# Channel-first partition order for the packed tap operand of a Conformer convolution (32 instead of 4 as the outermost dimension of its reads)

## The chip, the cores and the metric

The kernel runs on one core of a Trainium2 chip. The metric is the device time of one execution in microseconds (us), the median of several runs; lower is better. A second number, the span, is what the hardware profiler covers of one execution from its first to its last instruction.

## What is computed

A small diffusion backbone with two layers, one sequence of 1024 latent tokens and 256 context tokens, model width 1024, all in float32. Layer 0 mixes tokens with a Conformer convolution, layer 1 with windowed attention; each layer ends in a gated convolutional feed-forward part. Every sub-layer is preceded by an RMS norm and by shift, scale and gate values (the modulation, "ada" in the kernel), which are matrix products of the condition vectors. The change lies in the Conformer part:

```python
def conformer_conv(h, w_pw1, b_pw1, w_dw, b_dw, ln_g, ln_b, w_pw2, b_pw2):
    u = h @ w_pw1 + b_pw1
    a, g = jnp.split(u, 2, axis=-1)
    v = a * jax.nn.sigmoid(g)
    v = dwconv(v, w_dw, b_dw)              # per channel, 31 taps along the tokens
    v = jax.nn.silu(layernorm(v, ln_g, ln_b))
    return v @ w_pw2 + b_pw2
```

## The kernel before, in words

Channels lie on the 128 partitions, so the width of 1024 is 8 blocks of 128 ("channel" below means such a block, `c` from 0 to 7), and tokens lie along the free dimension: two tiles of 512 latent tokens (t = 0 and 1) and one of 256 context tokens (t = 2). Float32 products are made of three matmuls of a high and a low part (`mm3`, line 193); weights arrive in a tile `raw`, are split by ScalarE into `wh` (line 914) and by VectorE into `wl` (line 919).

The convolution stage is one loop over the channels (lines 988 to 1061), written out by hand: in `tc.manual_schedule` the order of the code is the order on TensorE, VectorE, ScalarE and GpSimd. The transfers, all issued by SyncE (SP), are ordered by a scheduler instead, and SP works its list strictly in order. A turn of the loop for channel `c` does this:

- It computes GLU of the next channel, `c + 1`, for the three token tiles: `glu_mm` on TensorE for the gate and the value half, `glu_gate` on ScalarE, `glu_mul` on VectorE, which writes the padded row `v`.
- The 31 taps of channel `c` are shared out. `NPE` of them (8 for channels 0 to 5, then 16 and 28) go to TensorE (`pe_taps`, matmuls at line 822), `NDV` (13, 13, 13, 13, 13, 13, 8, 0) to VectorE (`dve`, line 843), and the rest are products on ScalarE (line 848) added by GpSimd (line 849). VectorE adds onto what TensorE left in the accumulator `cacc`; `last` (line 853) adds the GpSimd part and frees `cacc`, of which there is one, for the next channel.
- For TensorE a matmul contracts over 128 partitions: 32 channels times 4 shifts of the token row. So that four shifted copies of a row stand on different partitions, `Shifted.load` (lines 795 to 805) stores `v` to a DRAM tile `v_dram` (line 799) and reads it back with four copies (line 792), one for each group of 32 channels, each with 4 shifts. The tile `vp` takes the front of the rows, `vpb` their end. The store of t = 0 is followed by reads into `vp`, that of t = 1 by more of `vp`, that of t = 2 by the reads into `vpb`. Each read waits on SP for its store to have landed.
- A modulation block of the layer is computed beside it (`ada_steps`): four pairs of matmuls (line 211), each with a 512 KB load of its own (`ld_ada`, line 109, into one of two `raw` buffers that the weight loads `w_load` use too), then a copy, transposes (line 223, the step `fin`) and a reduction on VectorE (line 226).

The source pattern of the reads is built here, with the shift outside and the channel inside:

```python
def rows_of(t, pitch, first, shift, n):
    return bass.AP(t.tensor, t.offset + first, [[shift, 4], [pitch, 32], [1, n]])
```

Partition 32 r + m therefore holds shift r of channel m. The tap weights must stand in the same order: `load_taps` (line 629) reads them with the same helper and a shift of 0, and `pack_taps` (line 638) picks with 12 ScalarE copies of 32 partitions each (line 647) the taps of each shift into `wpk`. Before the first channel's GLU, the prologue (lines 922 to 986) runs norm and modulation and packs the taps. The loaded tap tile has the buffer (`tag="vp"`) that the first reads into `vp` then take.

Of the kernel before, what the change touches and what calls it, by code (L numbers as in the profile page):

```python
# [8 lines left out]
F32 = mybir.dt.float32  # L9
# [9 lines left out]
P = 128  # L19
D = 1024  # L20
KC = D // P
# [8 lines left out]
TAPS = 31  # L30
# [5 lines left out]
NPE = (8, 8, 8, 8, 8, 8, 16, 28)  # L36
# [7 lines left out]
SEG = {}  # L44
# [4 lines left out]
NPAR = _o  # L49
# [3 lines left out]
def hybrid_dit_kernel(  # L53
# [4 lines left out]
    nc = tc.nc  # L58
# [31 lines left out]
    ident = const.tile([P, P], F32, name="ident")  # L90
# [291 lines left out]
    x = [None] * 3  # L382
# [208 lines left out]
    shift = pool(xst1, "shift", side="right")  # L591
# [17 lines left out]
    with ExitStack() as cs:  # L609
# [4 lines left out]
        cv = pool(cvs, "cv", 2)  # L614
# [3 lines left out]
        OOF = (0, 512, SEQ + PADW)  # L618
        rbt = pc.tile([P, 1536], F32, tag="cv", name="rbt")
        id4 = cv.tile([P, 32], F32, name="id4", bufs=1)  # L620
        nc.vector.tensor_reduce(out=id4, in_=ident.rearrange("p (r m) -> p m r", m=32),
                                axis=AX.X, op=ALU.add)
        wpk = cv.tile([P, SUM_M, 4], F32, name="wpk", bufs=1)

        def rows_of(t, pitch, first, shift, n):

            return bass.AP(t.tensor, t.offset + first, [[shift, 4], [pitch, 32], [1, n]])

        def load_taps():

            o, n = SEG["wdw"]
            w = cv.tile([P, 4, n], F32, tag="vp", name="wdw4", bufs=1)
            for g in range(4):
                nc.sync.dma_start(out=w[:, g],
                                  in_=rows_of(par, NPAR, 32 * g * NPAR + o, 0, n))
            return w

        def pack_taps(w):
            c0 = 0
            while c0 < KC:  # L640
                m = NPE[c0] // 4
                n = sum(x == NPE[c0] for x in NPE[c0:])
                o = sum(NPE[:c0]) // 4
                for r in range(4):
                    rows = slice(32 * r, 32 * r + 32)
                    src = w[rows].rearrange("p g (c t) -> p c t g", t=TAPS)
                    nc.scalar.copy(
                        out=wpk[rows, o:o + n * m, :].rearrange("p (c s) g -> p c s g", s=m),
                        in_=src[:, c0:c0 + n, m * r:m * r + m, :])
                c0 += n  # L650

        def ada_src(b, ks):
            return adaw[0, b, :, ks, :]
# [79 lines left out]
        def glu_mm(q, t, half, part=None):  # L733
            n = TOK[t][1]
            if part in (None, 0):
                q.ps[half] = pc.tile([P, 512], F32, tag="s", name="glu_ps", bufs=2)
            ops = unit_ops((q.wg, q.wa)[half], *x[t])
            if part is not None:
                ops = ops[4 * part:4 * part + 4]
            mm3(q.ps[half][:, :n], ops, part is not None, part in (None, 0), part in (None, 1),  # L740
                t == 2)
# [7 lines left out]
        def glu_mul(q, t):  # L749
            n = TOK[t][1]  # L750
            nc.vector.scalar_tensor_tensor(out=q.v[:, VOF[t]:VOF[t] + n], in0=q.ps[1][:, :n],
                                           scalar=seg("bpw1", q.c, 1), in1=q.sg[:, :n],
                                           op0=ALU.add, op1=ALU.mult)
# [111 lines left out]
        def run(steps, n):  # L865
            for _ in range(min(n, len(steps))):
                steps.pop(0)()
# [54 lines left out]
        with tc.manual_schedule(engines=CONV_ENGINES):  # L922
            load_next(True)
            stats(0)
            ada0(2)
            bcast_a(0)
            bcast_b(0)
            normalize_h(0)
            ada0(0)
            load_next(True)  # L930
            load_block(1)
            load_h(2, nc.sync)
            w4 = load_taps()
            apply(0, 0, 2)
            stats(1, nc.vector, 0, 4)
            apply(0, 2, 4)
            split_pending()
            split_pending()
            q = glu_begin(0)
            ada0(3)  # L940
            stats(1, nc.vector, 4, 8)
            glu_mm(q, 0, 0, 0)
            stats(2, nc.vector, 0, 4)
            stats(2, nc.vector, 4, 8)
            bcast_a(1)
            ada0(1)
            bcast_a(2)
            bcast_b(1)
            apply(0, 4, 6)
            apply(0, 6, 8)  # L950
            glu_mm(q, 0, 1, 0)
            glu_mm(q, 0, 0, 1)
            normalize_h(1)
            glu_mm(q, 0, 1, 1)
            apply(1, 0, 2)
            glu_out(q, 0)
            apply(1, 2, 4)
            bcast_b(2)
            glu_mm(q, 1, 0, 0)
            normalize_h(2)  # L960
            apply(1, 4, 6)
            apply(1, 6, 8)
            apply(2, 0, 4)
            apply(2, 4, 8)
            pack_taps(w4)
            dgs = tap_weights(0)
            glu_mm(q, 1, 1, 0)
            glu_mm(q, 1, 0, 1)
            glu_mm(q, 1, 1, 1)
            w_load()  # L970
            w_load()
            vp = Shifted(0, q.v)
            vp.load(0)
            glu_out(q, 1)
            vp.load(1)
            wh = w_hi()
            glu_mm(q, 2, 0)
            w_lo(wh)
            glu_mm(q, 2, 1)
            glu_out(q, 2)  # L980
            vp.load(2)
            w_lo(w_hi())
            ys = [make_h(t, "y") for t in range(3)]

            ld_ada(0, 0)
            ld_ada(0, 1)
            fin = None
            for c in range(KC):
                wide_taps = M[c] * P > 256
                if wide_taps:  # L990
                    dgs = tap_weights(c)
                r, taps = pe_taps(c, vp, dgs)
                first, pq, dq, last = conv_steps(c, q.v, r, NPE[c], NDV[c])
                ada_ps = pc.tile([P, 512], F32, tag="s", name="ada_ps", bufs=2) if c == KC - 1 else None
                ada = ada_steps(0, 4 + c, lambda u, c=c: araw[c, u], ada_ps)
                if c + 1 < KC:
                    q = glu_begin(c + 1)
                    glu_mm(q, 0, 0)
                    glu_gate(q, 0)
                    glu_mm(q, 0, 1)  # L1000
                    run(ada, 2)
                    ld_ada(c, 2)
                    ld_ada(c, 3)
                    run(taps, 4)
                    glu_mul(q, 0)
                    if fin:
                        fin()
                    first()
                    run(pq, 2)
                    vp = Shifted(c + 1, q.v)  # L1010
                    vp.load(0)
                    if c > 0:
                        ymean(c - 1)
                    glu_mm(q, 1, 0)
                    run(pq, 1)
                    glu_gate(q, 1)
                    run(ada, 2)
                    w_load()
                    w_load()
                    run(dq, 3)  # L1020
                    run(pq, 1)
                    glu_mm(q, 1, 1)
                    run(ada, 1)
                    run(dq, 3)
                    glu_mul(q, 1)
                    vp.load(1)
                    run(pq, 1)
                    if M[c + 1] * P <= 256:
                        dgs = tap_weights(c + 1)
                    wh = w_hi()  # L1030
                    glu_mm(q, 2, 0)
                    run(dq, 1)
                    w_lo(wh)
                    ld_ada(c + 1, 0)
                    run(pq, 1)
                    glu_gate(q, 2)
                    wh = w_hi()
                    glu_mm(q, 2, 1)
                    run(dq, 1)
                    glu_mul(q, 2)  # L1040
                    vp.load(2)
                    w_lo(wh)
                    ld_ada(c + 1, 1)
                    run(pq, 99)
                    run(dq, 99)
                    fin = ada.pop()
                else:
                    run(ada, 2)
                    ld_ada(c, 2)
                    ld_ada(c, 3)  # L1050
                    fin()
                    first()
                    run(pq, 99)
                    ymean(c - 1)
                    run(taps, 2)
                    run(ada, 3)
                    for i in range(4):
                        load_ada(i)
                    run(taps, 2)
                    run(dq, 99)  # L1060
                last()
# [3 lines left out]
        with tc.manual_schedule(engines=CONV_ENGINES):  # L1065
# [159 lines left out]
            for t in range(3):  # L1225
                n = TOK[t][1]
# [69 lines left out]
            for u in range(2, 2 * KC):  # L1296
                g, dc = divmod(u, KC)
                tiles = tiles_of(u)
                w = unit(("pw2", g, dc), 0)
# [534 lines left out]
```

## Time and profile before

| | before |
|---|---|
| device time, median of 3 runs | 2856.61 us (2853.77 to 2858.43) |
| the profiled execution, device time | 2854.5 us |
| its span | 2852.7 us |
| TensorE matmuls busy in the span | 2669.1 us, 94% |
| VectorE, ScalarE, GpSimd busy | 56%, 34%, 19% |
| chain that ended last: TensorE | 75% |
| chain that ended last: DMA | 9% (`vpb<-v_dram` 3%, `v_dram<-v` 3%) |

The page's chain is followed back from the last instruction: each piece is the work, or the wait, that released the next. TensorE carries three quarters of it, mostly in the two feed-forward parts. [...] The DMA share is the mean busy share of the core's 16 DMA engines. In a row of the timeline the bracket gives the idle time of that engine before the instruction and what ended it.

### The profile page before, as it was taken

What the parts mean: (1) busy time and instruction counts of PE and PEld (TensorE: products, weight loads), DVE (VectorE), ACT (ScalarE), POOL (GpSimd) and SP (SyncE); (2) the same over time, 40 slices, a digit from 0 to 9 for tenths busy, and PEclk for the clock granted to TensorE, in tenths of its full rate; (3) what the DMA queues carried; (4) which work ended last, traced back from release to release, by engine and by line L of the source; (5) the groups of instructions that cost most, each with busy time, mean ns of one, the idle gap of its engine ahead of it and who ended that gap; (6) DMA issues with size and microseconds to landing.
All of it is one profiled execution on the core that took longest, in us unless ns stands there. A gap on an engine that the chain in (4) does not pass through costs nothing.

```text
span 2852.7 us, 34110 instructions
## 1 busy us (share of the span) xinstructions
PE 2669.1 (94%) x13860; PEld 2155.7 (76%) x13860; DVE 1609.8 (56%) x2273; ACT 984.0 (34%) x1405; POOL 549.7 (19%) x384
## 2 busy tenths in 40 slices
PE   5888784999999999999999999899999999999997
PEld 3556561577888888888888788788878888888886
DVE  6346452545445445544544866998975455545546
ACT  6333321555221111222112524777752222222223
POOL 1365641332000000000000402556630000000003
PEclk8899997999999999999999999999999999999998
DMA  6444464532111111111111163233011111111111
GB/s 238 122 138 136 138 193 149 192 109 83 59 45 37 37 38 37 38 38 45 37 37 38 49 210 111 55 85 78 22 54 59 45 52 45 52 45 52 45 52 67
DMA packets 79421, 225.53 MB, mean 79 GB/s; under 512 B 8480, under 2 KB 20384, under 8 KB 76960
## 3 DMA queue, kind: packets, MB, share of 16 engines
q1 hardware_dynamic: 79264, 223.36, 24.4%
q8 instruction: 109, 1.79, 0.3%
q14 instruction: 48, 0.39, 0.0%
HBM read 202.17 MB, written 21.16 MB: 78 GB/s over the span
## 4 chain that ended last, share of the span: by engine, by line
PE 75%; DMA 9%; DVE 8%; ACT 5%; issue 2%; SPq 1%; POOL 1%; DVEq 0%; ACTq 0%; POOLq 0%
PE up_ps L193 37%; PE dn_ps L193 17%; DMA vpb<-v_dram 3%; DMA v_dram<-v 3%; PE glu_ps L193 3%; PE wo_ps L193 2%; PE pw_ps L193 2%; PE pB L193 2%; PE pA L193 2%; PE cacc L822 2%; PE tp L1545 1%; DVE tl L178 1%; PE v_ps L193 1%; SPq L792 1%; DVE mx L1523 1%
## 5 line engine op out<-in xcount | busy, mean ns | idle before, releaser
L131 DVE TENSOR_TENSOR wl<-raw,wh 128x1024 fp32r<-128x1024 f32 x165 | 204.7, 1241 | 515.5 <-issue 312.3
L193 PE MATMUL up_ps<-x_l,wh 128*128 128x512 f32 (+1 forms) x1760 | 415.3, 370 | 4.2 <-POOL x_l L322 4.2
L193 PE MATMUL up_ps<-x_h,wl 128*128 128x512 f32 (+1 forms) x1760 | 409.9, 369 | 0.2 <-ACT x_h L311 0.2
L193 PE MATMUL up_ps<-x_h,wh 128*128 128x512 f32 (+1 forms) x1760 | 408.3, 369 | 0.0
L193 PEld LDWEIGHTS up_ps<-x_l,wh 128*128 128x128 f32 x1760 | 312.1, 189 | 64.0 <-POOL x_l L322 5.8
L193 PEld LDWEIGHTS up_ps<-x_h,wh 128*128 128x128 f32 x1760 | 311.5, 189 | 55.7 <-issue 0.8
L193 PEld LDWEIGHTS up_ps<-x_h,wl 128*128 128x128 f32 x1760 | 310.7, 189 | 56.1 <-issue 0.8
L461 DVE SCALAR_TENSOR_TENSOR y<-dn_ps,mods,y 128x512 f32<-128x512 f32 (+1 forms) x400 | 270.2, 694 | 129.2 <-PE dn_ps L193 129.1
L257 POOL TENSOR_TENSOR acc<-acc,scrh 128x256 f32<-128x256 f32 (+1 forms) x36 | 37.4, 1039 | 1575.5 <-ACT scrh L256 1573.6
L416 ACT ACTIVATE c<-up_ps,pv 128x1282 f32<-128x1282 f32 (+1 forms) x88 | 115.6, 1315 | 588.3 <-PE up_ps L193 588.3
L129 ACT CAST wh<-raw 128x1024 fp32r<-128x1024 f32 x178 | 185.5, 1043 | 358.3 <-PE dn_ps L193 328.1
L193 PE MATMUL dn_ps<-gl,wh 128*128 128x512 f32 (+1 forms) x800 | 233.0, 373 | 0.7 <-DVE y L461 0.7
L193 PE MATMUL dn_ps<-gh,wl 128*128 128x512 f32 (+1 forms) x800 | 231.6, 371 | 0.0
L193 PE MATMUL dn_ps<-gh,wh 128*128 128x512 f32 (+1 forms) x800 | 231.3, 370 | 0.0
L849 POOL TENSOR_TENSOR a<-a,pr 128x1295 f32<-128x1295 f32 x62 | 190.2, 3068 | 174.8 <-ACT pr L848 171.8
L1539 POOL TENSOR_TENSOR p<-p,rd 128x640 f32<-128x640 f32 (+1 forms) x128 | 154.3, 1236 | 234.1 <-DVE rd L1537 173.0
L420 DVE SCALAR_TENSOR_TENSOR c<-up_ps,pv,c 128x1281 f32<-128x1281 f32 (+1 forms) x88 | 124.5, 1416 | 121.7 <-ACT c L416 121.7
L193 PEld LDWEIGHTS dn_ps<-gl,wh 128*128 128x128 f32 x800 | 142.9, 188 | 31.7 <-DVE y L461 6.4
L193 PEld LDWEIGHTS dn_ps<-gh,wh 128*128 128x128 f32 x800 | 145.2, 188 | 26.9
L193 PEld LDWEIGHTS dn_ps<-gh,wl 128*128 128x128 f32 x800 | 145.2, 188 | 26.8
L843 DVE SCALAR_TENSOR_TENSOR cacc<-v,pv,cacc 128x1295 f32<-128x1295 f32 x86 | 134.9, 1569 | 24.4 <-PE cacc L822 22.3
L424 DVE SCALAR_TENSOR_TENSOR c<-up_ps,pv,c 128x1281 f32<-128x1281 f32 (+1 forms) x88 | 124.5, 1415 | 2.3
(255 smaller groups left out, 4048.3 us busy)
## 6 DMA issues: line engine op xcount, KB each, us to landing
raw<-in_up_dram SPq DMA_DIRECT2D x88, 512.0 KB
ada<-in_adaw_dram SPq DMA_DIRECT2D x11, 2048.0 KB
raw<-in_down_dram SPq DMA_DIRECT2D x44, 512.0 KB
raw<-in_adaw_dram SPq DMA_DIRECT2D x38, 512.0 KB
raw<-in_pw_dram SPq DMA_DIRECT2D x32, 512.0 KB
vpb<-v_dram SPq DMA_DIRECT2D x32, 256.0 KB
qs<-q_dram SPq DMA_DIRECT2D x32, 256.0 KB
raw<-in_wo_dram SPq DMA_DIRECT2D x16, 512.0 KB
```

The source lines that it names most:

```text
L129: nc.scalar.copy(out=wh, in_=raw)
L131: lo_engine[0].tensor_sub(out=wl, in0=raw, in1=wh)
L193: nc.tensor.matmul(ps, lhsT=w, rhs=x, start=first and n == 0, stop=last and n == len(seq) - 1)
L257: (eng or nc.gpsimd).tensor_add(out=acc, in0=acc, in1=sq)
L416: nc.scalar.activation(out=c, in_=ps[:, :W], func=AF.Identity, bias=seg("fdb", l * 2 * NJ + ab * NJ + j, 1), scale=wd[1])
L420: nc.vector.scalar_tensor_tensor(out=c[:, 1:W], in0=ps[:, 0:W - 1], scalar=wd[0], in1=c[:, 1:W], op0=ALU.mult, op1=ALU.add)
L424: nc.vector.scalar_tensor_tensor(out=c[:, 0:W - 1], in0=ps[:, 1:W], scalar=wd[2], in1=c[:, 0:W - 1], op0=ALU.mult, op1=ALU.add)
L461: nc.vector.scalar_tensor_tensor(out=h, in0=ps[:, m * n:(m + 1) * n], scalar=mod(l, 5, dc, s), in1=h, op0=ALU.mult, op1=ALU.add)
L822: nc.tensor.matmul(r["acc"][32 * g:32 * g + 32, o:e], lhsT=w[:, (4 * s + g) * 32:(4 * s + g + 1) * 32], rhs=vp.rows(g, s, o, e - o), start ...
L843: nc.vector.scalar_tensor_tensor(out=acc, in0=v[:, j:j + OW], scalar=tap(j), in1=acc, op0=ALU.mult, op1=ALU.add)
L849: return lambda: nc.gpsimd.tensor_tensor(out=r["a2"], in0=r["a2"], in1=pr, op=ALU.add)
L1539: nc.gpsimd.tensor_tensor(out=it.p4[:, hh, :it.wid], in0=it.p4[:, hh, :it.wid], in1=rd[:, hh:hh + 1].to_broadcast([P, it.wid]), op=ALU.mult)
```

## The change

Three things are edited. The reads get the pattern channel outside (32), shift inside (4), so that partition 4 m + r holds shift r of channel m; the identity-like tile `id4` follows that order. The tap weights are loaded with the shift in the address, once for each run of channels with the same share of taps (`runs`: channels 0 to 5, 6, 7), which makes 12 loads of 4 and 3 packing copies over all 128 partitions out of 12. And in the turn of the loop a few steps change places: `glu_mul` of t = 0 and `fin` stand before the tap matmuls, the first pair of modulation matmuls and its two next loads behind them, and one ScalarE product moves ahead by one place.

```diff
--- before.py
+++ after.py
@@ -618,36 +618,36 @@
         OOF = (0, 512, SEQ + PADW)
         rbt = pc.tile([P, 1536], F32, tag="cv", name="rbt")
         id4 = cv.tile([P, 32], F32, name="id4", bufs=1)
-        nc.vector.tensor_reduce(out=id4, in_=ident.rearrange("p (r m) -> p m r", m=32),
+        nc.vector.tensor_reduce(out=id4, in_=ident.rearrange("p (m r) -> p m r", r=4),
                                 axis=AX.X, op=ALU.add)
         wpk = cv.tile([P, SUM_M, 4], F32, name="wpk", bufs=1)
 
+        runs = [(NPE.index(x), NPE.count(x), x // 4) for x in sorted(set(NPE))]
+
         def rows_of(t, pitch, first, shift, n):
 
-            return bass.AP(t.tensor, t.offset + first, [[shift, 4], [pitch, 32], [1, n]])
+
+            return bass.AP(t.tensor, t.offset + first, [[pitch, 32], [shift, 4], [1, n]])
 
         def load_taps():
 
-            o, n = SEG["wdw"]
-            w = cv.tile([P, 4, n], F32, tag="vp", name="wdw4", bufs=1)
-            for g in range(4):
-                nc.sync.dma_start(out=w[:, g],
-                                  in_=rows_of(par, NPAR, 32 * g * NPAR + o, 0, n))
+            o = SEG["wdw"][0]
+            w = cv.tile([P, 4, KC * TAPS], F32, tag="vp", name="wdw4", bufs=1)
+            for c0, n, m in runs:
+                e = (n - 1) * TAPS + m
+                for g in range(4):
+                    nc.sync.dma_start(
+                        out=w[:, g, c0 * TAPS:c0 * TAPS + e],
+                        in_=rows_of(par, NPAR, 32 * g * NPAR + o + c0 * TAPS, m, e))
             return w
 
         def pack_taps(w):
-            c0 = 0
-            while c0 < KC:
-                m = NPE[c0] // 4
-                n = sum(x == NPE[c0] for x in NPE[c0:])
+            for c0, n, m in runs:
                 o = sum(NPE[:c0]) // 4
-                for r in range(4):
-                    rows = slice(32 * r, 32 * r + 32)
-                    src = w[rows].rearrange("p g (c t) -> p c t g", t=TAPS)
-                    nc.scalar.copy(
-                        out=wpk[rows, o:o + n * m, :].rearrange("p (c s) g -> p c s g", s=m),
-                        in_=src[:, c0:c0 + n, m * r:m * r + m, :])
-                c0 += n
+                src = w.rearrange("p g (c t) -> p c t g", t=TAPS)
+                nc.scalar.copy(
+                    out=wpk[:, o:o + n * m, :].rearrange("p (c s) g -> p c s g", s=m),
+                    in_=src[:, c0:c0 + n, 0:m, :])
 
         def ada_src(b, ks):
             return adaw[0, b, :, ks, :]
@@ -998,13 +998,13 @@
                     glu_mm(q, 0, 0)
                     glu_gate(q, 0)
                     glu_mm(q, 0, 1)
+                    glu_mul(q, 0)
+                    if fin:
+                        fin()
+                    run(taps, 4)
                     run(ada, 2)
                     ld_ada(c, 2)
                     ld_ada(c, 3)
-                    run(taps, 4)
-                    glu_mul(q, 0)
-                    if fin:
-                        fin()
                     first()
                     run(pq, 2)
                     vp = Shifted(c + 1, q.v)
@@ -1012,13 +1012,12 @@
                     if c > 0:
                         ymean(c - 1)
                     glu_mm(q, 1, 0)
-                    run(pq, 1)
+                    run(pq, 2)
                     glu_gate(q, 1)
                     run(ada, 2)
                     w_load()
                     w_load()
                     run(dq, 3)
-                    run(pq, 1)
                     glu_mm(q, 1, 1)
                     run(ada, 1)
                     run(dq, 3)
```

**SP, the queue of transfers, one turn** (from the reads of one channel's `vpb` to those of the next; numbers in tile names tell tiles apart and differ between the two builds). `raw<-in_adaw` is a modulation load, `raw<-in_pw` a weight load. Before:

```order
L792 DMA vpb<-v_dram_1399 128x1x512 x4
L109 DMA raw<-in_adaw_dram 128x1024 x2
L799 DMA v_dram_1704<-v 128x527
L792 DMA vp<-v_dram_1704 128x1x512 x4
L109 DMA raw<-in_pw_dram 128x1024 x2
L799 DMA v_dram_1704<-v 128x527
L792 DMA vp<-v_dram_1704 128x1x273 x4
L109 DMA raw<-in_adaw_dram 128x1024
L799 DMA v_dram_1704<-v 128x271
L109 DMA raw<-in_adaw_dram 128x1024
L792 DMA vpb<-v_dram_1704 128x1x512 x4
```

The same stretch with the change:

```order
L792 DMA vpb<-v_dram_1398 128x1x512 x4
L799 DMA v_dram_1703<-v 128x527
L792 DMA vp<-v_dram_1703 128x1x512 x4
L109 DMA raw<-in_adaw_dram 128x1024 x2
L109 DMA raw<-in_pw_dram 128x1024 x2
L799 DMA v_dram_1703<-v 128x527
L792 DMA vp<-v_dram_1703 128x1x273 x4
L109 DMA raw<-in_adaw_dram 128x1024
L799 DMA v_dram_1703<-v 128x271
L109 DMA raw<-in_adaw_dram 128x1024
L792 DMA vpb<-v_dram_1703 128x1x512 x4
```

Two modulation loads move behind the first store and the first four reads of the next channel; the rest keeps its place.

**TensorE, around the taps of one channel.** `glu_ps` is the end of GLU for t = 0 of the next channel, `ada_ps` a modulation pair, `cacc` the taps, `ada_pt` the transposes, `ymean` the sums for the layer norm. Before:

```order
L193 MATMUL glu_ps<-xh_249,wh 128x512 x8
L211 MATMUL ada_ps<-raw,c_80 32x512 x4
L822 MATMUL cacc<-vp,dg 32x512 x8
L822 MATMUL cacc<-vp,dg 32x272 x8
L822 MATMUL cacc<-vpb,dg 32x240 x8
L822 MATMUL cacc<-vpb,dg 32x271 x8
L223 MATMUL ada_pt<-ident,ada_sb 128x128 x4
L862 MATMUL ymean<-y_678,ones_88 32x512
```

With the change:

```order
L193 MATMUL glu_ps<-xh_257,wh 128x512 x8
L223 MATMUL ada_pt<-ident,ada_sb 128x128 x4
L822 MATMUL cacc<-vp,dg 32x512 x8
L822 MATMUL cacc<-vp,dg 32x272 x8
L822 MATMUL cacc<-vpb,dg 32x240 x8
L822 MATMUL cacc<-vpb,dg 32x271 x8
L211 MATMUL ada_ps<-raw,c_80 32x512 x4
L862 MATMUL ymean<-y_677,ones_88 32x512
```

The transposes and the modulation pair have changed places around the taps. VectorE's list has the same rows in the same order as before.

## Rows read from the trace of the kernel before

**Rows 1.** Stretches: from:to, us, busy PE PEld DVE ACT POOL, clock, DMA share, GB/s

```profile
120.00:356.00 236.00, 199.11 (x1162) 138.53 (x1162) 134.56 (x113) 86.71 (x80) 142.50 (x65) 0.93 0.47 138
356.00:485.00 129.00, 87.55 (x662) 55.83 (x661) 46.06 (x42) 29.32 (x28) 46.17 (x19) 0.81 0.57 173
```

**Rows 2.** Chain of waits, one turn (start, us, what)

```profile
209.56 3.62 PE cacc L822 x26
213.17 0.59 PE ada_pt L223 x4
...
220.41 0.99 PE ada_ps L211 x8
...
228.01 3.37 DMA v_dram<-v
...
234.22 8.38 DMA v_dram<-v
...
242.62 0.54 SPq L792
...
244.32 13.18 DMA vpb<-v_dram
...
257.54 3.56 PE cacc L822 x26
```

**Rows 3.** Short stretches, columns as in rows 1

```profile
13.00:20.00 7.00, 3.59 (x17) 0.58 (x18) 4.84 (x7) 4.96 (x10) 0.00 (x0) 1.00 1.01 412
...
254.00:257.00 3.00, 1.01 (x2) 0.18 (x2) 0.00 (x0) 0.00 (x0) 2.92 (x2) 0.51 0.26 99
...
1864.00:1866.00 2.00, 2.00 (x16) 1.73 (x14) 1.97 (x4) 0.59 (x1) 1.75 (x2) 1.00 1.06 213
```

**Rows 4.** Timeline of TensorE in that turn, and channel 6's first taps

```profile
232.67 2.00 PE L193 MATMUL glu_ps<-xl,wh 128*128 128x512 f32 x8
...
243.67 1.22 PE L211 MATMUL ada_ps<-raw,c 128*32 128x512 f32 x8
246.71 2.85 PE L822 MATMUL cacc<-vp,dg 128*32 128x512 f32 x32 [1.82 <-issue]
...
388.87 5.49 PE L822 MATMUL cacc<-vp,dg 128*32 128x512 f32 x64 [1.15 <-POOL v L730]
```

**Rows 5.** Timeline of VectorE in that turn

```profile
227.19 0.75 DVE L751 SCALAR_TENSOR_TENSOR v<-glu_ps,pv,sg 128x512 f32<-128x512 f32 x1 [3.48 <-PE glu_ps L193]
...
230.48 1.22 DVE L919 TENSOR_TENSOR wl<-raw,wh 128x1024 fp32r<-128x1024 f32 x1 [1.06 <-ACT wh L914]
...
244.99 1.62 DVE L853 TENSOR_TENSOR y<-cacc,a 128x512 f32<-128x512 f32 x3 [1.12 <-POOL v L730]
```

**Rows 6.** Timeline of the start, until the first channel's taps end

```profile
31.45 11.00 SPq L634 DMA_DIRECT2D wdw<-in_par_dram  x4
...
73.87 3.02 ACT L647 COPY wpk<-wdw 32x48 f32<-32x48 f32 x12
...
95.12 1.98 PE L193 MATMUL glu_ps<-xh,wh 128*128 128x512 f32 x8
...
116.55 3.61 PE L822 MATMUL cacc<-vpb,dg 128*32 128x240 f32 x26 [1.62 <-DMA vpb<-v_dram]
```

**Rows 7.** Chain of waits, from channel 5's last taps to the stage's end

```profile
352.21 3.62 PE cacc L822 x26
...
403.27 5.79 PE cacc L822 x58
...
423.90 14.25 DMA v_dram<-v
...
446.54 17.40 DMA raw<-in_adaw_dram
...
468.81 9.27 PE cacc L822 x100
...
478.94 6.21 PE cacc L822 x101
```

## The prediction, made before the changed kernel was run

> **What bounds the kernel now.** The table of stretches comes first [rows 1]. From 120 to 356 us TensorE is busy for 199.11 of 236 us at a granted clock of 0.93, and from 356 to 485 for 87.55 of 129 at 0.81. So some 78 us of idle TensorE time, and more at a lowered clock, lie in the convolution; that is what can be won.
>
> The chain of waits of one turn of the channel loop says what the idle time waits for [rows 2]. The last tap matmuls of a channel end at 209.56 + 3.62 = 213.18 us, those of the next channel at 257.54 + 3.56 = 261.10: a turn of 47.9 us. In it lie a store `v_dram<-v` of 8.38 us, and from the issue of the four `vpb` reads at 242.62 until the matmuls go on at 257.54 another 14.9 us. A store earlier in the turn landed in 3.37 us; the one of 8.38 stands behind four tap reads.
>
> Why these are slow is in the DMA columns of short stretches [rows 3]. While only the tap reads run (254 to 257 us) the share is 0.26 and the rate 99 GB/s: a quarter of the 16 engines, 24 GB/s for each of them. Whole-width loads at 13 to 20 us show 1.01 and 412 GB/s, 26 GB/s for each. The reads are short of engines, not of speed, and they are the only large copies here whose source pattern begins with a dimension of 4. Other copies of this kernel begin with 32 rows (the reads of `k_dram` and `q_dram` in attention): at 1864 to 1866 us they keep a share of 1.06, all engines, at 213 GB/s. So 32 is enough to use all engines.
>
> **Rate of the new reads.** A group of four is 1 MB. At 24 GB/s on each of 16 engines it takes 2.7 us, at the 213 GB/s of the 32-row copies 4.9 us; now it takes 10.6 at 99 GB/s. I take 2.7, because the destination is the same 128 partitions that gets 24 GB/s per engine today, and keep 4.9 as the slow end. [...]
>
> **One turn after the change**, counted from the end of a channel's taps.
>
> TensorE: from 213.18 to the end of the second pair of modulation matmuls at 243.67 + 1.22 = 244.89 it works without a gap, 31.7 us [rows 2, 4]. The change reorders this work but keeps its amount. Then come the taps: the first two parts, 784 columns, took 2.85 us [rows 4]; the last two, 511 columns, took 3.56 with most of their wait at a clock of 0.51 [rows 2, 3], and at the first parts' speed (they came straight behind other work) 2.85 × 511 / 784 = 1.86. Taps 4.7 us, TensorE 36.4 us per turn.
>
> VectorE: it needs the finished taps, runs the 13 remaining taps, and its last additions, ending at 244.99 + 1.62 = 246.61, free the accumulator for the next taps. That is 33.4 us after the taps. In it are waits of 3.48 us for TensorE, 1.06 for a weight load and 1.12 for GpSimd [rows 5]. The first stays and grows by 0.4, as the modulation pair (0.99) now stands where the transposes (0.59) stood. The second is a load that queued behind tap reads and goes. The third goes too: the ScalarE products come one earlier and are no longer held up by late weights. 33.4 + 0.4 - 1.1 - 1.1 = 31.6, with the taps 36.4. Both engines give the same turn.
>
> Do the transfers stay behind that? The last store of a turn is issued 234.22 - 213.18 = 21.0 us after the taps [rows 2]. It lands in 3.4 us plus 2.7 for the half megabytes of tap reads and modulation weights ahead of it: 27.1. Four issues (1.7 us from the first to the last now, and half a microsecond) and a landing like the store's give 32.7. The first matmul that needs it stands at 31.7 + 2.85 = 34.5. Hidden, by 1.8 us; at the slow rate it is 0.4 late.
>
> A new wait: two modulation loads that stood ahead of the next channel's first tap reads on SP now stand behind them, and weight loads are queued right behind those. The reads can start about 1 us before the taps end, the 2 MB of both groups take 5.3 us (7.5 at the slow rate), and landing adds one or two: 5.5 to 8.5 us. TensorE wants them at 220.41 - 213.18 + 0.4 = 7.6 [rows 2]. The wait is 0 to 1 us, after which GLU, both later stores and the weight loads would be late by as much. I take a turn of 37.5 us, bounds 36.4 and 41.
>
> **Start, until the first channel's taps end** (now 116.55 + 3.61 = 120.16 us [rows 6]). Packing the taps takes 12 ScalarE copies in 3.02 us, 0.25 each; three copies over all partitions take 0.8, or 1.5 if each costs double. The last copy frees the buffer that the first tap reads want, and ScalarE is the chain there, so all behind it moves up by 2.2 (1.5). GLU of channel 1 then ends at 95.12 + 1.98 - 2.2 = 94.9, and taps of 4.7 follow: 99.6. The transfers must be through by 94.9 + 2.85. From 74.7 on: reads issued by 77.0, a store landed by 81 behind them, reads issued by 83.3, the last store landed by 89 behind those, reads issued by 91, landed by 95. Saved: 20.6 us; 14 if the transfers come nine later.
>
> The tap loads become 12 in place of 4, eight of them with 16 or 28 bytes in a row. The four took SP 11.00 us from 31.45 on; 12 at that price end at 64.5, packing begins at 73.87 [rows 6]. I cost them at nothing; past 43 us they would push everything.
>
> **Five turns**, up to 352.21 + 3.62 = 355.83 [rows 7]: 235.7 now, 187.5 then. Saved 48.2 (bounds 31 and 53.7).
>
> **Sixth turn**: channel 6 has twice the taps on TensorE (first parts 5.49 us [rows 4], so 9.0 in all, 4.3 more). It ends at 403.27 + 5.79 = 409.06 [rows 7], so it takes 53.2 now and 41.8 then. Saved 11.4 (8 to 12.6).
>
> **Tail**, to 478.94 + 6.21 = 485.15 [rows 7]: 76.1 us. A store of 14.25 and a modulation load of 17.40 are on the chain, both queued with tap reads and 2 MB loads [rows 7]. After the change GLU of channel 7 ends 232.67 - 213.18 + 0.4 = 19.9 us after the taps [rows 4]; the last modulation load still stands behind the reads on SP and lands at about 31.5. Then modulation, transposes and means (2.6), taps 9.27, modulation 0.6, taps 6.21: 50. Saved 26.1; 16 if that load lands as late as now relative to its issue, 30 if it hides better.
>
> **Sum**: 20.6 + 48.2 + 11.4 + 26.1 = 106.3 us off the profiled execution's 2854.5, so **2748 us**. That execution is 2.1 below the median of the runs shown, 2856.61, which the range covers. Behind 485 us nothing is changed; the 2 MB loads for the next stage are issued at the same places and have room, since all transfers of the conv stage shrink more than the stage does. With the bounds: 14 + 31 + 8 + 16 = 69, and 21.5 + 53.7 + 12.6 + 30 = 118.
>
> **Rivals.**
> (a) The new order of loads makes the turn. If the modulation pair lands 4 us late in each turn, it is 40 to 41 us: five turns and the sixth save 22 less, the tail some 5 less, 2770 to 2788. For: the waiting line on SP is in order, and a weight load in the present turn holds up ScalarE and VectorE. Against: the arithmetic above. Chance 0.2.
> (b) All waits hide and the turn is the 36.4 us of the engines, with a shorter tail: 2736 or below. Chance 0.08.
> (c) Slower: the reads gain nothing, because the copies still run on a quarter of the engines, or because the source cannot give more than 100 GB/s. Then the modulation pair, which ran in the shade of the tap wait, comes out of it, 7 × 1.0 us, and its next loads queue behind 1 MB of slow reads: -1 + 10.6 + 2.6 = 12.2 us against 7.6, 4.6 late in six turns, 27 us. With 2 us back from packing: 2854.5 + 7 + 27 - 2 = about 2886. It decides as soon as a group of reads needs 10 us or more. Against: 24 GB/s per engine now, and the 32-row copies on all engines [rows 3]; but no row has a source of 32 against a destination of 128. [...] Chance 0.04.
>
> **How the numbers follow.** Forecast 0.66, (a) 0.2, (b) 0.08, (c) 0.04, and 0.02 for something near no change. A difference of 0.2%, 6 us, is about what a measurement of this kernel can tell. Faster: 0.94. Within: 0.02. Slower: 0.04. The range from 2734 to 2788 takes in the forecast's bounds and nearly all of (a); it leaves out (c) and the end of (b).
>
> **What would show it.** Right: stretches with tap reads alone at a DMA share well over 0.26; stores of 2.5 to 6 us; taps of 4.7 us at clock 1.00 without gaps; turns of 36.5 to 38; the first taps ending at about 100 us, the stage at about 379. Wrong: a share of 0.26 again (c), TensorE waiting for modulation loads in every turn (a), packing or the first reads held up by SP at 65 us or later, or time lost after the stage, where 2 MB loads would be waited for.

## The result, and the profile after

The changed kernel takes 2769.68 us (median of 4 runs, 2767.78 to 2774.87), the kernel before 2855.73 beside it: a ratio of 0.9701, 95% interval 0.9684 to 0.9718. The profiled execution took 2768.97 us; its span is 2767.2 and the mean granted clock of TensorE, as a share of full speed, 0.986, against 2852.7 and 0.973. Of the 106.3 us of the forecast 85.5 came.

The stretches of the changed kernel that answer to [rows 1] and [rows 3]: from the first channel's last tap to the sixth's, from there to the end of the stage, and two short ones in which mostly tap reads run (columns as in rows 1).

```profile
96.00:301.00 205.00, 190.19 (x1168) 137.58 (x1164) 145.27 (x115) 86.75 (x79) 139.11 (x64) 0.96 0.50 159
301.00:403.00 102.00, 87.04 (x677) 55.24 (x670) 48.73 (x41) 31.42 (x29) 51.52 (x22) 0.90 0.66 228
206.00:208.00 2.00, 2.00 (x10) 1.68 (x9) 1.93 (x3) 0.00 (x0) 2.00 (x1) 1.00 0.93 332
219.00:221.00 2.00, 2.00 (x16) 0.69 (x9) 1.96 (x2) 0.92 (x1) 2.00 (x1) 1.00 0.92 304
```

The reads now keep all 16 engines busy: a share of 0.92 to 0.93 where it was 0.26, and over 300 GB/s where it was 99. But TensorE still idles for 14.8 us in the five turns (12.2 in front of the taps, 2.6 in front of modulation matmuls whose load was late), and a turn takes 41.0 us (205.1 / 5), not the 37.5 of the forecast. The chain of waits of one turn, which answers to [rows 2], tells why.

```profile
176.85 0.92 PE cacc L822 x16
177.76 0.92 PE ada_ps L211 x8
...
179.28 7.06 DMA raw<-in_adaw_dram
...
186.38 1.05 PE ada_ps L211 x4
187.43 11.47 PE glu_ps L193 x72
...
199.40 3.54 DVE wl L919
202.94 1.49 DVE cacc L843
...
211.12 1.56 issue
212.68 6.26 PE cacc L822 x64
```

No `v_dram` store and no `vpb` read is on it any more. In the first half the chain waits for the second modulation pair's load, then it goes over TensorE to VectorE: a weight remainder `wl` of 3.54 us, five taps, the last additions, and only then the next taps on TensorE. The "issue" from 211.12 on lies inside VectorE's last additions (210.96 to 212.58 below); for the sixth turn the trace names them as what TensorE waited for. TensorE had been done for 2.44 us by then, as its timeline shows (first taps of this turn, then of the sixth), and what followed ran slowly.

```profile
212.68 4.54 PE L822 MATMUL cacc<-vp,dg 128*32 128x512 f32 x32 [2.44 <-issue]
...
336.65 8.45 PE L822 MATMUL cacc<-vp,dg 128*32 128x512 f32 x64 [2.96 <-DVE y L853]
```

The first two parts took 4.54 us where [rows 4] show 2.85 for the same work; the mean granted clock from 212.7 to 217.2 us is 0.62 (0.50 from 213.7 to 215.7), and from 217.2 to 219 it is 1.00. VectorE in the same turn, answering to [rows 5], and two rows of GpSimd:

```profile
193.25 0.75 DVE L751 SCALAR_TENSOR_TENSOR v<-glu_ps,pv,sg 128x512 f32<-128x512 f32 x1 [5.82 <-PE glu_ps L193]
...
195.38 1.72 DVE L919 TENSOR_TENSOR wl<-raw,wh 128x1024 fp32r<-128x1024 f32 x1
...
199.40 3.54 DVE L919 TENSOR_TENSOR wl<-raw,wh 128x1024 fp32r<-128x1024 f32 x1
...
210.96 1.62 DVE L853 TENSOR_TENSOR y<-cacc,a 128x512 f32<-128x512 f32 x3
...
193.02 3.00 POOL L849 TENSOR_TENSOR a<-a,pr 128x1295 f32<-128x1295 f32 x1
...
198.88 10.00 POOL L849 TENSOR_TENSOR a<-a,pr 128x1295 f32<-128x1295 f32 x3 [2.85 <-ACT pr L848]
```

VectorE idles 5.82 us in front of the GLU multiply of the second tile, and behind it has work without a gap of note until the taps can go on. The second `wl` begins 0.5 us after a GpSimd addition; 3.54 us is that addition's remaining 2.5 and about 1.1 of its own. The first one ends 197.10, that is 1.08 after the addition that was running (193.02 + 3.00). Both rows read as if a subtraction stood still until the addition is through; why it would, no run here shows. VectorE's 13 taps of this turn kept their 1.56 to 1.57 us each beside the same additions.

Where the start was won (timeline of ScalarE, SP and TensorE; answers to [rows 6]):

```profile
31.12 14.84 SPq L639 DMA_DIRECT2D wdw<-in_par_dram  x12
...
73.61 0.52 ACT L648 COPY wpk<-wdw 128x48 f32<-128x48 f32 x3
...
91.62 2.84 PE L822 MATMUL cacc<-vp,dg 128*32 128x512 f32 x32
94.28 1.91 PE L822 MATMUL cacc<-vpb,dg 128*32 128x240 f32 x32
```

And the sixth turn's taps and the tail in the chain of waits (answers to [rows 7]):

```profile
336.65 11.90 PE cacc L822 x111
...
374.53 6.66 DMA raw<-in_adaw_dram
...
386.06 9.59 PE cacc L822 x99
...
396.52 6.21 PE cacc L822 x111
```

### The profile page after: what moved, and what is told of

Read it like the earlier page. It is cut to its first block, busy times and chain, and to the rows that moved or that the text cites. A ratio compares the mean times of both kernels' runs of the same rounds, so it can differ in the third digit from the quotient of the medians.

```text
span 2767.2 us, 34117 instructions
## 1 busy us (share of the span) xinstructions
PE 2646.0 (96%) x13860; PEld 2145.8 (78%) x13860; DVE 1622.0 (59%) x2273; ACT 984.5 (36%) x1396; POOL 549.5 (20%) x384
## 3 DMA queue, kind: packets, MB, share of 16 engines
HBM read 202.00 MB, written 21.16 MB: 81 GB/s over the span
## 4 chain that ended last, share of the span: by engine, by line
PE 78%; DVE 10%; ACT 5%; DMA 3%; issue 2%; POOL 1%; SPq 1%; DVEq 0%; ACTq 0%; POOLq 0%
PE up_ps L193 38%; PE dn_ps L193 18%; PE glu_ps L193 4%; PE wo_ps L193 3%; PE cacc L822 2%; PE pw_ps L193 2%; DVE cacc L843 2%; PE pB L193 2%; DMA raw<-in_adaw_dram 2%; PE pA L193 2%; PE tp L1544 1%; DVE tl L178 1%; PE v_ps L193 1%; PE ada_ps L211 1%; DVE mx L1522 1%
## 5 line engine op out<-in xcount | busy, mean ns | idle before, releaser
L257 POOL TENSOR_TENSOR acc<-acc,scrh 128x256 f32<-128x256 f32 (+1 forms) x36 | 37.5, 1041 | 1574.1 <-ACT scrh L256 1572.3
```

What stands on the lines that cost most here:

```text
L257: (eng or nc.gpsimd).tensor_add(out=acc, in0=acc, in1=sq)
```

## The experiments

The theory after this reading: the reads are no longer the limit; VectorE's order of work makes the turn, TensorE's gap before the taps costs clock on top, and the new order of the loop is no help. The rivals: the order is what made the fast reads pay; or the late modulation loads make the turn (rival (a) of the prediction); or GpSimd does. In the table a turn is the mean of the five after the first channel, from the end of its taps; the gap is TensorE's idle time before a turn's taps; "slow" counts, of five turns, those whose first tap parts took over 4 us instead of 2.85.

| kernel | us (median) | ratio to before, 95% | turn | gap | slow |
|---|---|---|---|---|---|
| the change | 2769.68 | 0.9701 (0.9684 to 0.9718) | 41.0 | 2.44 | 5 |
| old reads, new order | 2895.79 | 1.0146 (1.0131 to 1.0161) | 53.8 | 2.46 | 2 |
| new reads, old order | 2758.77 | 0.9662 (0.9648 to 0.9676) | 38.7 | 2.2 | 2 |
| modulation pair later | 2770.64 | 0.9705 (0.9689 to 0.9721) | 40.7 | 2.9 | 2 |
| remainder on GpSimd | 2752.99 | 0.9638 (0.9622 to 0.9654) | 38.0 | 0.58 | 0 |
| reads in halves | 2764.74 | 0.9683 (0.9666 to 0.9699) | 40.6 | 2.46 | 4 |
| VectorE taps earlier | 2751.66 | 0.9626 (0.9611 to 0.9640) | 37.7 | 0.39 | 0 |
| mixed order | 2749.00 | 0.9616 (0.9602 to 0.9630) | 37.1 | 1.30 | 0 |
| mixed, remainder on GpSimd | 2739.49 | 0.9584 (0.9570 to 0.9598) | 35.8 | 0, once 0.29 | 0 |
| mixed, taps and products earlier | 2740.07 | 0.9585 (0.9569 to 0.9601) | 35.8 | 0 | 0 |
| mixed, with both | 2739.76 | 0.9595 (0.9581 to 0.9609) | 35.8 | 0 | 0 |

The gap alone doesn't decide about the clock: behind 2.9 us the taps were slow in two turns of five, behind 2.44 us in all five (granted clock 0.62 to 0.65 in these).

### The order of the loop alone, and the reads alone

Old reads with the new order: the kernel before with

```diff
+                    glu_mul(q, 0)
+                    if fin:
+                        fin()
+                    run(taps, 4)
                     run(ada, 2)
                     ld_ada(c, 2)
                     ld_ada(c, 3)
-                    run(taps, 4)
-                    glu_mul(q, 0)
-                    if fin:
-                        fin()
...
-                    run(pq, 1)
+                    run(pq, 2)
...
-                    run(pq, 1)
```

> The kernel before with only the new order of the channel loop; the reads keep 4 as their outermost dimension. Theory (the reads' rate is the cause, the order is worth nothing without it): the share of the DMA engines in stretches with tap reads alone stays 0.26; the modulation pair comes out of the shade of the tap wait and its loads queue behind slow reads, 4 to 5 us late in each turn: 2870 to 2890 us, with 2886 as worked out for rival (c) of the prediction. Rival (the order of loads gives much of the gain, since the tap reads no longer queue behind 1 MB of modulation weights): 2835 us or less.

Measured 2895.79, 10 us beyond that estimate and 6 beyond its range. TensorE waits for the modulation pair behind the slow reads, 5.4 to 8.2 us in each of the five turns where 4 to 5 were expected (one of them in the timeline), and the share of a stretch with reads alone is 0.26 as before (table of stretches):

```profile
238.61 3.16 PE L211 MATMUL ada_ps<-raw,c 128*32 128x512 f32 x8 [8.22 <-DMA raw<-in_adaw_dram]
```

```profile
108.00:112.00 4.00, 1.69 (x4) 0.18 (x2) 0.00 (x0) 0.00 (x0) 0.00 (x0) 0.50 0.26 94
```

So the order alone costs some 40 us; it gives none of the gain. The other half, the changed kernel with the same lines put back:

> The changed kernel with the channel loop in its former order (modulation pair, its two next loads, then taps, GLU multiply, transposes; products 2, 1, 1); the new partition order, loads and packing stay. Theory (the engine order of VectorE makes the turn of 41.0 us, and the reads have all the gain): the modulation loads stand ahead of the tap reads again, so the late pair costs nothing (1.2 us less), the first pair fills part of the 2.44 us gap of TensorE before the taps, so that these run at full clock (1.5 less), and VectorE waits for the transposes behind the taps (0.9 more): a turn near 39.2 us, six turns 11 less, about 2758 us (2750 to 2766). Rival (the reordering is needed, since the 1 MB of modulation weights ahead of the tap reads makes the last store and the last reads late): TensorE waits for vpb again by 2 us or more in each turn, 2780 us or more.

Measured 2758.77, the time that the theory gave, 11 us faster than the whole change; but the taps came at full clock in three turns of five only, and the gap stayed at 2.2 us. Its timeline (TensorE, then VectorE):

```profile
165.90 4.47 PE L822 MATMUL cacc<-vp,dg 128*32 128x512 f32 x32 [2.23 <-issue]
...
205.95 2.84 PE L822 MATMUL cacc<-vp,dg 128*32 128x512 f32 x32 [2.23 <-issue]
...
211.14 0.19 DVE L226 TENSOR_REDUCE mods<-ada_pt 128x8 f32<-128x32 f32 x1 [4.64 <-PE ada_pt L223]
```

With the same gap of 2.23 us the taps run slowly in one turn (granted clock 0.62 from 165.9 to 170.3 us) and at full clock in the next (1.00 from 206 to 208.6). No TensorE wait for `vpb` appeared, so fast reads don't need the new order. What this order loses is VectorE's wait for the transposes behind the taps: it starts its taps at 211.73, 1.36 us after TensorE's last (210.37).

### The modulation pair by itself

```diff
-                    run(ada, 2)
                     w_load()
                     w_load()
                     run(dq, 3)
                     glu_mm(q, 1, 1)
+                    run(ada, 2)
                     run(ada, 1)
```

> The changed kernel with the second modulation pair of a turn behind the GLU matmuls of the second token tile instead of ahead of them. Theory (the pair's loads land late, the 8 matmuls take 2.24 us instead of 1.06, and this sits on the way to VectorE's GLU multiply, on which the turn hangs): the pair takes 1.06, GLU multiply comes 2.2 us earlier on TensorE's side, the turn falls by 1.2 to 2.3 us, six turns 7 to 14: 2756 to 2762 us. The gap of TensorE before the taps stays near 2.4 us and the taps at 6.2 us. Rival (TensorE or the transfers make the turn): within 3 us of the changed kernel.

Measured 2770.64: no gain, yet not for the rival's reason. Timeline of VectorE and of ScalarE:

```profile
188.29 0.75 DVE L751 SCALAR_TENSOR_TENSOR v<-glu_ps,pv,sg 128x512 f32<-128x512 f32 x1 [3.25 <-PE glu_ps L193]
...
194.86 1.23 DVE L919 TENSOR_TENSOR wl<-raw,wh 128x1024 fp32r<-128x1024 f32 x1 [4.34 <-ACT wh L914]
...
193.78 1.05 ACT L914 CAST wh<-raw 128x1024 fp32r<-128x1024 f32 x1 [2.64 <-DMA raw<-in_pw_dram]
```

The multiply does come earlier, 12.9 us after the last taps' end instead of 15.5. But SP, whose order the scheduler sets, now issues the two weight loads behind that multiply's store, at 189.53, which is 14.2 us after the taps' end; in the changed kernel they stand ahead of that store, at 186.21, 8.5 us after the taps' end. Their cast waits for the data, and VectorE for the cast, 4.34 us. The run moved a wait along VectorE's chain; the price of the late pair stays open in it.

### The weight remainder

```diff
-        def w_lo(wh):
+        def w_lo(wh, eng=nc.vector):
             wl = wpool.tile([P, 1024], F32R, tag="wl", name="wl")
-            nc.vector.tensor_sub(out=wl, in0=wraw.pop(0), in1=wh)
+            eng.tensor_sub(out=wl, in0=wraw.pop(0), in1=wh)
...
-                    w_lo(wh)
+                    w_lo(wh, nc.gpsimd)
```

> The changed kernel with the second of the two weight remainders of a turn computed by GpSimd instead of VectorE. Theory (VectorE's subtraction of 3.54 us is 1.2 us of work and 2.3 us of waiting until a GpSimd addition that began before it has ended; VectorE's chain makes the turn): VectorE's chain gets 3.5 us shorter, the additions on GpSimd then end last, at about the same time as now, so last additions come some 2 us earlier, TensorE's gap before the taps falls under 1 us and the taps run at full clock in 4.7 us: a turn of about 37.7 us, six turns 20 less, near 2750 us. GpSimd's three additions behind it take 9.1 us instead of 10.0. Rival (the subtraction is slow for its own sake, or GpSimd makes the turn): GpSimd's chain grows by the 2.5 us of the subtraction, the last additions wait for it, 2768 us or more.

Measured 2752.99, 17 us less. Timeline of GpSimd, VectorE and TensorE:

```profile
185.62 3.00 POOL L849 TENSOR_TENSOR a<-a,pr 128x1295 f32<-128x1295 f32 x1
190.13 2.42 POOL L919 TENSOR_TENSOR wl<-raw,wh 128x1024 fp32r<-128x1024 f32 x1 [1.51 <-ACT wh L914]
192.50 9.15 POOL L849 TENSOR_TENSOR a<-a,pr 128x1295 f32<-128x1295 f32 x3
...
187.97 1.72 DVE L919 TENSOR_TENSOR wl<-raw,wh 128x1024 fp32r<-128x1024 f32 x1
201.68 1.62 DVE L853 TENSOR_TENSOR y<-cacc,a 128x512 f32<-128x512 f32 x3 [1.70 <-POOL a L849]
...
203.40 2.84 PE L822 MATMUL cacc<-vp,dg 128*32 128x512 f32 x32 [0.57 <-PE ada_pt L223]
```

The three additions fall from 10.00 to 9.15 us once no subtraction stands between them, and the remaining subtraction on VectorE ends 1.07 us after the addition that ran when it began (185.62 + 3.00). The gap falls to 0.57 and the taps of all five turns run at full clock (2.84 us for the first parts here, granted clock 1.00 from 120 to 280 us). GpSimd is now last, as expected.

### Reads cut in halves

Each tap read as two copies of 16 channels by 4 shifts.

> The changed kernel with each of its tap reads cut into two copies of 16 channels by 4 shifts (64 partitions), so that the outermost dimension of each is 16. Theory (16 are enough for all 16 engines; what is lost is the issue of 8 copies in place of 4, 2.4 us on SP for each group): stretches with reads alone keep a share of 0.7 or more and over 200 GB/s; the modulation pair behind the reads on SP lands 2.4 us later, and with it VectorE's GLU multiply: six turns 10 to 15 us more, 2778 to 2786 us. Rival (16 rows reach only half of the engines): a share of 0.5 or less in those stretches and the last reads late, 2795 us or more. Rival (nothing in the turn hangs on the reads any more): 2772 us or less.

Measured 2764.74: the third case. SP's timeline and the DMA issues of the stretch 196 to 216 us (queue, count, KB each, us to landing):

```profile
180.39 1.01 SPq L109 DMA_DIRECT2D raw<-in_adaw_dram  x2
181.45 2.43 SPq L793 DMA_DIRECT2D vp<-v_dram  x4
...
207.43 5.22 SPq L793 DMA_DIRECT2D vpb<-v_dram  x8
```

```profile
vpb<-v_dram SPq DMA_DIRECT2D x8, 128.0 KB, 2.7
```

Eight copies of 128 KB are issued in 5.22 us and each lands 2.7 us after its issue, some 200 GB/s, the pace of the issues. That is twice the 99 GB/s that the old reads, four copies of a group together, got. So more than the old quarter of the engines (a share of 0.26) serves these copies with 16 outermost; whether all 16 do, a run bound by issues can't tell (the share from 208 to 213 us is 0.58, short of the 0.7 expected). The forecast of later modulation loads was wrong because the scheduler put them between the two halves (180.39). And 2.4 us more for each group cost nothing: nothing in a turn hangs on the tap reads.

### VectorE's order

Changed kernel, three taps ahead of the multiply:

```diff
                     run(ada, 1)
-                    run(dq, 3)
+                    run(dq, 6)
                     glu_mul(q, 1)
```

> The changed kernel with three of VectorE's 13 taps of a turn taken ahead of the GLU multiply of the second token tile, into the 5.82 us in which VectorE waits for that tile's matmuls. Theory (VectorE's order makes the turn of 41.0 us): the multiply stays where it is, since 4.7 us fit into 5.8; VectorE's chain behind it gets 4.7 us shorter, GpSimd's last addition (208.88 of the turn that ends at 218.94) then decides, 2 us earlier than now; TensorE's gap before the taps falls to about 0.5 us and the taps run at full clock: 2.1 + 1.5 = 3.6 us per turn, six turns 21 less, about 2748 us (2745 to 2755). Rival (the late modulation pair makes the turn): no gain, 2767 us or more. Rival (GpSimd's additions and the weight remainders collide longer): 2756 to 2765.

Measured 2751.66, as the theory had it: 18 us with the same instructions and the same transfers, three taps of VectorE standing earlier. Timeline of VectorE, then TensorE:

```profile
171.77 14.43 DVE L843 SCALAR_TENSOR_TENSOR cacc<-v,pv,cacc 128x1295 f32<-128x1295 f32 x9 [3.77 <-PE cacc L822]
187.03 0.75 DVE L751 SCALAR_TENSOR_TENSOR v<-glu_ps,pv,sg 128x512 f32<-128x512 f32 x1 [0.83 <-PE glu_ps L193]
...
202.69 1.62 DVE L853 TENSOR_TENSOR y<-cacc,a 128x512 f32<-128x512 f32 x3 [2.87 <-POOL v L730]
...
204.41 2.84 PE L822 MATMUL cacc<-vp,dg 128*32 128x512 f32 x32 [0.39 <-issue]
```

The idle 5.82 us in front of the multiply are 0.83, and VectorE now waits 2.87 us for GpSimd before its last additions. This settles that VectorE's order makes the turn of the changed kernel. The late modulation pair is still there and still takes 2.18 us of TensorE in this turn (179.01 to 181.19); in the last kernels below it takes 0.99. So its price is about 1.2 us of TensorE's time a turn.

### A version that beats both

Modulation pair and loads ahead, but multiply and transposes ahead of the taps too:

```diff
+                    run(ada, 2)
+                    ld_ada(c, 2)
+                    ld_ada(c, 3)
                     glu_mul(q, 0)
                     if fin:
                         fin()
                     run(taps, 4)
-                    run(ada, 2)
-                    ld_ada(c, 2)
-                    ld_ada(c, 3)
```

> The changed kernel with the modulation pair and its two next loads again ahead of the taps, but GLU multiply and transposes kept ahead of the taps too. From the run with the former loop order (2758.77 us; its turn of 38.4 us, or 40.1 where the taps ran at half clock, in turn about). Theory: the 0.65 us of transposes move into TensorE's gap of 2.2 us, VectorE no longer waits for them behind the taps (1.4 us, from 210.37 to 211.73), and with a gap of 1.6 us all taps run at full clock: a turn of 37.0, six turns 8 to 11 less, 2747 to 2751 us. Rival (VectorE is bound elsewhere and only the wait is moved): 2756 us or more.

Measured 2749.00, inside its range, with a turn of 37.1 us and a gap of 1.30. To it, the remainder on GpSimd:

> The kernel of the run h1 with the second weight remainder of a turn on GpSimd. Theory: VectorE's chain gets another 2.1 us shorter; TensorE's gap (1.6 us) closes and TensorE is then the bound, with a turn of 36.2 to 36.6 us (38.4 less 2.23 of gap): 2743 to 2747 us. Rival (GpSimd's chain, 2.4 us longer, ends last): 2750 us or more.

or, instead, two taps and two products earlier (`run(dq, 5)` for the second `run(dq, 3)`, `run(pq, 3)` and `run(pq, 2)` for the second `run(pq, 2)` and the `run(pq, 1)` behind it):

> The kernel of the run h1 with two of VectorE's taps ahead of the GLU multiply of the second tile, and two ScalarE products with their GpSimd additions two places earlier, so that neither engine idles before that multiply. Theory: VectorE's chain gets 2 to 3 us shorter and GpSimd ends 6 us earlier, TensorE is the bound: a turn of 36.2 to 36.6 us, 2743 to 2747 us. Rival (the GLU multiply comes later behind the taps, its store too, and the reads land late): TensorE waits for vpb, 2752 us or more.

or both:

> The kernel of the run h1 with both aids at once: the second weight remainder on GpSimd, and two VectorE taps and two products earlier. Theory (with either aid TensorE is already the bound of the turn, 35.9 us without a gap, so together they give nothing more): 2736 to 2741 us, within 3 us of either. Rival (a wait is left in some turns that both together remove): 2734 us or less.

Measured 2739.49, 2740.07 and 2739.76, some 3 us below the ranges expected of the single aids (a turn of 35.8 us where 36.2 to 36.6 were expected), and inside that of both. The chain of waits of the kernel with the remainder on GpSimd is TensorE alone from one turn's taps to the next:

```profile
166.06 0.84 PE ymean L862 x4
166.91 5.68 PE glu_ps L193 x24
172.59 0.99 PE ada_ps L211 x8
173.59 22.33 PE glu_ps L193 x120
195.92 1.00 PE ada_ps L211 x8
197.50 4.50 PE cacc L822 x64
```

TensorE is the bound, 35.94 us a turn (166.06 to 202.00), and either aid gets there; together they add nothing. These three are 30 us below the change and 115 to 120 below the kernel before as it ran beside them.

## Why the prediction was right, and where it was not

The forecast was 2748 us; measured 2769.68, inside the range (2734 to 2788) and faster, as the largest chance said. The cause, reads that use all engines, was right. That the range held is in part luck: its slow end rests on turns of 41 us from loads that land late, and the turns came to 41.0 for mostly other reasons. By its steps, in the profiled executions:

| step | forecast saving | measured |
|---|---|---|
| start, to the first taps' end | 20.6 | 24.0 |
| five turns | 48.2 | 30.5 |
| sixth turn | 11.4 | 6.0 |
| tail | 26.1 | 21.9 |
| behind the stage | 0 | 3.1 |

- **The reads.** Right: all engines (a share of 0.92 and 0.93), and 300 GB/s or more (304 and 332). A group at 332 GB/s is 3.2 us, between the 2.7 taken and the 4.9 of the slow end. For a source of 32 against a destination of 128, of which rival (c) had no row, the share of 0.93 is now one.
- **The transfers stay hidden.** Right: all that TensorE still waits for `vp` or `vpb` is 0.3 us of one weight load, and reads issued over 2.4 us longer cost nothing.
- **The start.** Packing took 0.52 us, below its 0.8, and TensorE's wait for ScalarE there fell from 3.54 to 0.95 us; the GLU matmuls behind it then took 1.12 to 1.22 us a group instead of up to 2.08 (granted clock 1.00 from 74 to 80 us, where it had been 0.50 from 77 to 83), a gain that the sum had left out. SP's 12 tap loads (14.84 us) stayed hidden, as said.
- **The turn: the failed step.** "Both engines give the same turn", 36.4 us. TensorE does, or better (35.94 with its gaps gone). VectorE does not: 34.8 us from the taps' end to its last addition (177.76 to 212.58) where the text had 31.6. Three terms were mis-sized. The multiply stands 15.5 us behind the taps instead of 14.4, the late modulation pair: in this turn its second half ran alone, after its load (186.38), so the pair took 2.24 us instead of 0.99; here the 1.1 us that the forecast allowed above 36.4 was right. The two weight remainders took 5.26 us (1.72 + 3.54) where the trace before had 1.22 + 2.47 and the text carried them over unchanged: a 1.6 us that depends on when a GpSimd addition begins. And a wait of 0.41 for TensorE came in.
- **Taps at 4.7 us.** Wrong in the turns, 6.0 to 6.3, right at the start (91.62 to 96.19). The forecast assumed that they come straight behind other work, although its own row [rows 4] has 1.82 us of idle time in front of the 2.85. VectorE being later than TensorE leaves a gap of 2.44 us, and in all five turns the clock was low after it (0.62 to 0.65 over the first two parts): 1.5 us a turn, though gaps as long were not always followed by it (table). With 36.4 + 1.1 + 1.6 + 0.4 + 1.5 the turn is 41.0. The sixth turn loses by the same; its taps took 11.90 us, at a mean clock of 0.75, for 9.0.
- **The tail: steps at full clock.** It missed by 4.2 us. The last modulation load landed 32.7 us after the taps (381.19) where 31.5 was forecast. The modulation, transposes and means behind it took 4.9 us (to 386.06) where 2.6 was forecast: TensorE had idled 9.1 us for that load, and its granted clock was then 0.50 (columns below as in rows 1). The rows of before had the same 4.9 us (463.94 to 468.81 in [rows 7]), also at 0.50.

```profile
381.00:386.00 5.00, 4.76 (x21) 1.65 (x25) 0.36 (x2) 0.00 (x0) 0.75 (x1) 0.50 0.99 416
```

- **The reordering.** The prediction costed it as the price of a late pair, 0 to 1 us a turn. It was never asked whether the old order was better with fast reads. It was, by 11 us.
- **Rival (a)** had the size of a turn (40 to 41 us; 2770 to 2788 in all) with a quarter of its cause: of the 4.6 us that a turn has above 36.4 the late pair makes 1.1 by the rows above. **Rival (b)**, 2736 or below when all waits hide, is nearly what the last three kernels reach. **Rival (c)** did not occur; the old reads with the new order show that its price was, if anything, too low.

## What to carry to other kernels

When a wait of 10 us goes, compare the order of every in-order engine with what is now early and late: here one changed count (three taps moved) was worth 18 us, where the whole change was worth 86. Work that has no deadline (taps, products) belongs in front of the instruction that waits, as much as fits into its wait. And an edit that reorders and an edit that speeds up should be timed apart: this reordering cost 11 us beside fast reads and 40 beside slow ones.

## What was not expected

- A VectorE subtraction of 1.22 us took up to 3.55 beside GpSimd additions (3.95 in the run with the old order), ending 1.0 to 1.1 us after the addition under way; moving it away shortened three GpSimd additions by 0.85 us.
- In the five turns of each kernel, TensorE's gaps of up to 1.82 us before the taps were followed by full speed (two kernels with 0.4 to 0.6, one with 1.30, [rows 4] with 1.82); gaps of 2.2 to 2.9 us by full speed or by a lowered clock, in the same kernel and with the same gap (2.23 us; first parts of 4.47 us at 0.62 and of 2.84 at 1.00). Which of the two comes is not settled.
- Behind the stage nothing was changed, yet the changed kernel's profile took 2364.5 us there, the kernel before 2367.5, and the eight kernels whose stage ended before 396 us 2368.6 to 2370.6. Most of this is the clock. In 40 us that begin 180 us behind the end of the stage, TensorE was busy for 35.9 us in every one of them; its granted clock was 1.00 in the changed kernel (first row below, columns as in rows 1), 0.91 in the kernel before and 0.90 to 0.92 in all experiments with the new reads, of which the second row is one (mixed, remainder on GpSimd). By an estimate from these clocks (40 × 0.09) that is up to 3.6 us. So the 3.1 us of the step "behind the stage" can be put down to the clock of this one execution; why it stayed high there is open, and so are the 1 to 3 us by which the eight lie above the kernel before.

```profile
582.73:622.73 40.00, 35.90 (x192) 28.55 (x191) 23.68 (x36) 18.61 (x29) 8.15 (x7) 1.00 0.16 53
547.73:587.73 40.00, 35.91 (x179) 28.34 (x179) 21.71 (x34) 18.48 (x27) 7.94 (x7) 0.91 0.15 51
```
